# A hybrid attention layer whose kernel schedules itself: the schedule learns of the port that VectorE and GpSimd share, and its TensorE prices are set anew

## The chip, the cores and the metric

The kernel runs on one core of one Trainium2 chip. Its engines are TensorE (PE in the profile, its weight loads PEld), VectorE (DVE), ScalarE (ACT), GpSimd (POOL) and SyncE (SP), which issues the DMAs. Each engine works through its own list of instructions in order and waits for others through semaphores. The metric is device microseconds of one execution, the median of the runs shown.

## What is computed

One decoder layer over 512 tokens of 1024 features, in fp32. Cut to what matters here:

```python
h = rmsnorm(x, ln_mix_g)
dq, dk, dv, nq, kc, vc, ksl, vsl, kwn, vwn, ng, mg = split(h @ w_in)
dq, dk, nq, ksl, kwn = (rope(rmsnorm(z)) for each)
y_diff = rmsnorm((softmax(q0 k0) - lam * softmax(q1 k1)) @ v)          # 8 heads, causal
k_cmp, v_cmp = (gelu(blocks(z + pos) @ w1) @ w2 for z in (kc, vc))     # 31 blocks
y_nsa = g0 * att(nq, k_cmp, v_cmp) + g1 * att(nq, ksl, vsl) + g2 * att(nq, kwn, vwn)   # 16 heads
mixed = sigmoid(mg0) * (y_diff @ w_proj_diff) + sigmoid(mg1) * (y_nsa @ w_proj_nsa)
x = x + mixed @ w_out
x = x + square(relu(rmsnorm(x) @ w_mlp_up)) @ w_mlp_down
```

## The kernel before

**Work and tiles.** Every large product is done with operands split in two: `hi` is the value rounded to fp32r and `lo` the remainder, and a product is three matmuls, hi·hi, hi·lo and lo·hi. Weights come in 157 pieces of 128 x 1024 (tile `wraw`, by DMA). `WStream.get` (L372) splits each piece in halves of 512 columns: a copy writes `whi` (ACT or DVE, whichever is free first by the schedule), and a subtraction writes `wlo` (DVE or POOL, likewise). Pieces are split one ahead of their use and loaded two ahead.

**Stages.** The input is normalised and transposed (`hn`, `hTh`, `hTl`). Then four streams run at once with a filler: `rope_stream` (L873) normalises and turns queries and keys (`norm_rope`, L811: tiles `sqr`, `str`, `t1r`, `t2r`, `rw`), transposes them on PE (`ptp`) and splits them; `score_stream` (L1014) makes scores (`sb`), maxima and exponentials (`p`, statistics `sm` and `smn`); `value_stream` (L1146) transposes probabilities (`pta`, `ptn`), splits them (`ah`, `al`) and multiplies them with values (`av`, `avn`); a side stream does the compressed keys and values (`hb`, `ob`). The filler writes the large projections (`gb`, weights stationary or moving), one chunk after the other. After the attention come the projections, the output product and the MLP, in banks `gb` and `ga` in turn.

**What sets the order.** Nothing is issued while the kernel is written out. Each call is noted by `Sched.note` (L190) with what it reads and writes, the engines that could do it, and a price in ns for each (`price`, L163). `Pe.run` (L72) takes steps of the streams by falling priority and advances its own clock `pe.now` by the price of each matmul (`mm`, L438, and `tr`, L442). At the end `Sched.flush` (L256) plays a list schedule: a clock for each engine, and at each step the engine that could start first takes, of what is ready, the instruction of the highest priority. An instruction with two possible engines goes to the one that gets to it first. The instructions are then issued in the order of the planned starts, so these prices decide both each engine's order and who does the splits. The step that takes an instruction is

```python
p, op = heapq.heappop(ok[e])
op.eng = e
op.start, op.end = t, t + op.ways[e][1]
self.free[e] = op.end
```

In it each engine's clock is its own: no instruction of one engine makes another's take longer. Nearly every instruction is issued from one line of `flush`, so the profile names them by their tiles; all have line L326.

Of the kernel before, what the change touches and what calls it, by code (L numbers as in the profile page):

```python
# [26 lines left out]
# how long (ns) a result of other engines takes to be there  # L27
S_LAT, P_LAT, T_LAT = 1000, 4000, 2000
# how much later (ns) than usual it may come without holding up what was put after it
SLACK = 250  # L30
# what a task yields at the end of a piece of weights
PIECE = 1e-3

# columns of w_in
# [4 lines left out]
# columns of the table of shape constants  # L39
# [25 lines left out]
class Pe:  # L65
    """The tensor engine's clock (ns) as the kernel is written out: its instructions are issued in the order
    written, so a task is written on when what it waits for should be there."""
# [4 lines left out]
    def run(self, tasks):  # L72
        """tasks: generators by falling priority. They yield a time to wait (ns), or a condition."""
# [20 lines left out]
class Engine:  # L94
    """Takes down the instructions of one engine."""
# [9 lines left out]
class Pool:  # L105
    """A tile pool whose buffers the schedule knows."""
# [20 lines left out]
class Op:  # L127
    __slots__ = ("eng", "ways", "a", "k", "prio", "deps", "users", "bufs", "left", "ready", "start", "end", "dma")


class Sched:
    """Instructions are taken down in the order the kernel is written, with what each reads and writes. A clock
    per engine and the usual price of each instruction then say which goes next: of those that are ready the one
    that is hot, then the one written first. In this order they are issued."""
# [5 lines left out]
    def __init__(self, nc):  # L140
        self.nc, self.tiles, self.ops, self.hot = nc, {}, [], False
        self.engs = {"ACT": nc.scalar, "DVE": nc.vector, "POOL": nc.gpsimd}
        self.free = {e: 0.0 for e in ("PE", "ACT", "DVE", "POOL", "SP")}
        self.hw = self.dma = 0.0
        self.count = 0
        self.held, self.queue = {}, {}
# [3 lines left out]
    def lat(self, p, c, reads):  # L150
        """from the end of p to the start of c; reads: c reads what p has written"""
# [11 lines left out]
    def price(self, eng, method, aps, k):  # L163
# [4 lines left out]
        if eng == "PE":  # L168
            if method == "transpose":
                return 109.0  # L170
            return max(107.0, 3 + self.size(aps[-1]) * 0.4167)
# [17 lines left out]

    def note(self, ways, a, k):  # L190
        """ways: engine, method and its function, of each engine that could do it"""
# [5 lines left out]
        op.ways = {e: (fn, self.price(e, m, aps, k)) for e, m, fn in ways}  # L197
        op.dma = None
# [57 lines left out]
    def flush(self):  # L256
        """issues what has been taken down"""
# [33 lines left out]
        while len(done) < len(ops):  # L291
# [14 lines left out]
            p, op = heapq.heappop(ok[e])  # L306
            op.eng = e
            op.start, op.end = t, t + op.ways[e][1]
# [21 lines left out]
class When:  # L330
    """Something that is there from a time on."""
# [11 lines left out]
class Slots:  # L343
    """Buffers of a pool: taken only when the last reader of an older one is written out."""
# [17 lines left out]
class WStream:  # L362
    """Weights in the order of use: loaded two pieces ahead, split one piece ahead."""
# [32 lines left out]
def hybrid_block(ctx: ExitStack, tc: tile.TileContext, x, ln_mix_g, w_in, dqg, dkg, lq1, lk1, lq2, lk2,  # L396
# [25 lines left out]
    # ------------------------------------------------------------------ helpers  # L422
# [8 lines left out]
    def split(hi, lo, src, hi_engs=("ACT", "DVE"), lo_engs=("DVE",)):  # L431
        """src = hi + lo, each short enough for one pass of the tensor engine"""
# [5 lines left out]
    def mm(out, lhsT, rhs, n, start, stop):  # L438
        T.matmul(out, lhsT=lhsT, rhs=rhs, start=start, stop=stop)
        pe.now += max(107.0, n * 0.4219)  # L440

    def tr(out, src):  # L442
        T.transpose(out, src, ident)
        pe.now += 109.0
# [3 lines left out]
    def rows(w, c0, n=512):  # L448
        """pieces of 256 rows, n columns from c0"""
# [5 lines left out]
    def segs(w, c0, strides, n):  # L455
        """pieces of 256 rows, runs of n columns from c0, at the strides ((stride, count), ...) from each other"""
# [15 lines left out]
    def gemm_tm(banks, xh, xl, nk=KT, mark=False, by_bank=0, n=512, per=2):  # L472
        """banks[t] = x[t] @ w ; x given as lhsT slices [128 k, 128 tokens], w n wide, per slices of k a piece;
        the last by_bank pieces bank by bank"""
# [1138 lines left out]
```

## Time and profile before

| what | value |
|---|---|
| median of 3 runs | 1117.32 us |
| the three runs | 1117.01 to 1119.86 us |
| profiled execution, first to last instruction | 1117.1 us |
| PE busy, share of the span | 1066.3 us, 95% |
| DVE busy | 802.3 us, 72% |
| ACT busy | 464.9 us, 42% |
| POOL busy | 415.4 us, 37% |
| mean granted TensorE clock | 0.997 |

How to read it: the busy time of an engine is the union of its instructions' times. A matmul's end is modelled and overlaps the next one's start, so a busy PE is not yet one that issues as fast as it can. The engines work on stages with different limits, so a share over the whole span says little; the windows by stage and the waits say more. The profiled execution is 0.2 us from the median of the runs, so its sums can be held against that median.

### The profile page before, as it was taken

What the parts mean: (1) busy time and instruction counts of PE and PEld (TensorE: products, weight loads), DVE (VectorE), ACT (ScalarE), POOL (GpSimd) and SP (SyncE); (2) the same over time, 40 slices, a digit from 0 to 9 for tenths busy, and PEclk for the clock granted to TensorE, in tenths of its full rate; (3) what the DMA queues carried; (4) which work ended last, traced back from release to release, by engine and by line L of the source; (5) the groups of instructions that cost most, each with busy time, mean ns of one, the idle gap of its engine ahead of it and who ended that gap; (6) DMA issues with size and microseconds to landing.
All of it is one profiled execution on the core that took longest, in us unless ns stands there. A gap on an engine that the chain in (4) does not pass through costs nothing.

```text
span 1117.1 us, 15775 instructions
## 1 busy us (share of the span) xinstructions
PE 1066.3 (95%) x5257; PEld 873.5 (78%) x5257; DVE 802.3 (72%) x1961; ACT 464.9 (42%) x1132; POOL 415.4 (37%) x416
## 2 busy tenths in 40 slices
PE   6999989999899999999999999999999999999998
PEld 5777867779677778777788887787888888888887
DVE  7788599999888999999999998657454233445232
ACT  4256245655454365565465564313332111233110
POOL 3714478338647271073211112322322222222321
PEclk9999999999999999999999999999999999999999
DMA  6354355542653324526345344642322233333232
GB/s 206 97 148 118 113 151 149 152 129 71 164 153 94 85 69 132 142 85 199 122 134 170 100 155 134 225 138 90 94 94 95 95 98 104 101 95 95 94 132 75
DMA packets 83905, 136.76 MB, mean 122 GB/s; under 512 B 8816, under 2 KB 33904, under 8 KB 83824
## 3 DMA queue, kind: packets, MB, share of 16 engines
q1 hardware_dynamic: 83824, 135.77, 40.2%
q8 instruction: 41, 0.67, 0.3%
q14 instruction: 40, 0.33, 0.1%
HBM read 106.64 MB, written 14.42 MB: 108 GB/s over the span
## 4 chain that ended last, share of the span: by engine, by line
PE 62%; DVE 22%; POOL 5%; DMA 5%; issue 3%; ACT 2%; SPq 1%; DVEq 0%; ACTq 0%; POOLq 0%
PE gb L326 31%; PE ga L326 21%; DVE p L326 5%; PE sb L326 3%; DMA kk<-kp 3%; PE avn L326 3%; DVE wlo L326 2%; POOL str L326 2%; PE ptn L326 2%; DVE al L326 2%; DVE rw L326 1%; DVE t1r L326 1%; POOL t1r L326 1%; DMA wraw<-in_w_in_dram 1%; PE hb L326 1%
## 5 line engine op out<-in xcount | busy, mean ns | idle before, releaser
L326 POOL TENSOR_TENSOR wlo<-wraw,whi 128x512 fp32r<-128x512 f32 (+1 forms) x163 | 237.7, 1461 | 596.8 <-ACT whi L326 386.9
L326 ACT CAST whi<-wraw 128x512 fp32r<-128x512 f32 (+1 forms) x203 | 121.8, 618 | 327.6 <-PE gb L326 158.5
L326 DVE CAST whi<-wraw 128x512 fp32r<-128x512 f32 x111 | 49.9, 451 | 198.2 <-PE ga L326 87.1
L326 DVE TENSOR_TENSOR wlo<-wraw,whi 128x512 fp32r<-128x512 f32 x151 | 130.4, 865 | 8.6 <-ACT whi L326 2.2
L326 PE MATMUL gb<-whi,hTh 128*128 128x512 f32 (+2 forms) x352 | 133.5, 388 | 2.2 <-ACT hTh L326 1.3
L326 PE MATMUL gb<-wlo,hTh 128*128 128x512 f32 (+2 forms) x352 | 135.1, 385 | 0.0
L326 PE MATMUL gb<-whi,hTl 128*128 128x512 f32 (+2 forms) x352 | 134.5, 383 | 0.4 <-DVE hTl L326 0.4
L326 DVE CUSTOM_DVE_ANT_0 p<-sb,cst 128x512 f32<-128x512 f32 (+2 forms) x192 | 91.8, 480 | 4.5 <-PE sb L326 3.3
L326 ACT ACTIVATE p<-p,smn 128x512 f32<-128x512 f32 (+3 forms) x128 | 71.9, 562 | 34.6 <-DVE smn L326 33.8
L326 PEld LDWEIGHTS gb<-whi,hTh 128*128 128x128 f32 x352 | 67.1, 192 | 12.5 <-ACT hTh L326 1.8
L326 PEld LDWEIGHTS gb<-whi,hTl 128*128 128x128 f32 x352 | 67.3, 192 | 10.8 <-DVE hTl L326 1.4
L326 PEld LDWEIGHTS gb<-wlo,hTh 128*128 128x128 f32 x352 | 67.6, 192 | 9.4 <-DVE wlo L326 0.3
L326 PE MATMUL gb<-big,whi 128*128 128x512 f32 x192 | 66.9, 407 | 0.0
L326 DVE TENSOR_SCALAR p<-p,smn,gates 128x512 f32<-128x512 f32 (+3 forms) x128 | 65.4, 515 | 1.5
L326 ACT CAST ah<-ptn 128x128 fp32r<-128x128 f32 (+3 forms) x101 | 42.8, 427 | 54.5 <-PE ptn L326 43.8
L326 PE MATMUL gb<-hTh,whi 128*128 128x512 f32 x160 | 64.6, 404 | 0.6 <-DVE t0t L326 0.4
L326 PE MATMUL gb<-hTl,whi 128*128 128x512 f32 x160 | 64.9, 406 | 0.0
L326 PE MATMUL ptn<-cst,p 128*128 128x128 f32 x320 | 60.4, 276 | 4.5 <-DVE al L326 1.4
L326 PE MATMUL gb<-hTh,wlo 128*128 128x512 f32 x160 | 64.5, 405 | 0.0
L326 PE MATMUL ga<-h2h,whi 128*128 128x512 f32 x160 | 62.4, 391 | 0.5 <-DVE x L326 0.5
L326 PE MATMUL ga<-h2l,whi 128*128 128x512 f32 x160 | 62.5, 390 | 0.0
L326 PE MATMUL ga<-h2h,wlo 128*128 128x512 f32 x160 | 62.2, 390 | 0.0
(250 smaller groups left out, 2631.5 us busy)
## 6 DMA issues: line engine op xcount, KB each, us to landing
wraw<-in_w_in_dram SPq DMA_DIRECT2D x36, 512.0 KB, 3.6
wraw<-in_w_mlp_up_dram SPq DMA_DIRECT2D x32, 512.0 KB, 3.8
wraw<-in_w_mlp_down_dram SPq DMA_DIRECT2D x32, 512.0 KB, 3.6
kk<-kp SPq DMA_DIRECT2D x48, 256.0 KB, 4.5
wraw<-in_w_in_dram SPq DMA_DIRECT2D x36, 256.0 KB, 3.1
big<-yd SPq DMA_DIRECT2D x16, 512.0 KB, 4.0
yd<-yo SPq DMA_DIRECT2D x8, 512.0 KB, 3.2
wraw<-in_w_proj_diff_dram SPq DMA_DIRECT2D x8, 512.0 KB, 3.8
```

Of the source, the lines that this page charges most:

```text
L326: op.ways[op.eng][0](*op.a, **op.k)
```

## The change

The schedule gets a sixth clock, `self.port`. A new function `ported` names the instructions that hold the SBUF port which DVE and POOL share: on POOL all but powers, on DVE four methods when no operand is in PSUM, and neither when all operands are under 64 elements wide. In `flush` an instruction that holds the port and finds it taken is put off: the next ready instruction of that engine that doesn't need the port goes first, and if there is none, the first starts when the port is free. The prices of PE in `price`, and the same in `mm` and `tr` for `pe.now`, become those of the second set of numbers. All else of the diff takes out comments and docstrings, whose lines stay blank or go, so that the line of the issued instructions is L357 in the kernel after.

```diff
@@ class Sched
-        self.hw = self.dma = 0.0
+        self.hw = self.dma = self.port = 0.0
...
             if method == "transpose":
-                return 109.0
-            return max(107.0, 3 + self.size(aps[-1]) * 0.4167)
+                return 113.0
+            return max(113.0, 5.5 + self.size(aps[-1]) * 0.4315)
...
+    TWICE = ("tensor_tensor", "tensor_scalar", "scalar_tensor_tensor", "tensor_copy")
+
+    def ported(self, eng, method, aps, k):
+
+        if max(self.size(x) for x in aps) < 64:
+            return False
+        if eng == "POOL":
+            return k.get("op") != OP.pow
+        return eng == "DVE" and method in self.TWICE and not any(
+            self.tiles[x.tensor.name].space == "PSUM" for x in aps if x.tensor.name in self.tiles)
...
             p, op = heapq.heappop(ok[e])
+            if op.port[e] and self.port > t:
+                put_off = [(p, op)]
+                while ok[e] and put_off[-1][1].port[e]:
+                    z = heapq.heappop(ok[e])
+                    if z[1].left == 0:
+                        put_off.append(z)
+                if not put_off[-1][1].port[e]:
+                    p, op = put_off.pop()
+                else:
+                    p, op = put_off.pop(0)
+                for z in put_off:
+                    heapq.heappush(ok[e], z)
             op.eng = e
-            op.start, op.end = t, t + op.ways[e][1]
+            op.start = max(t, self.port) if op.port[e] else t
+            op.end = op.start + op.ways[e][1]
+            if op.port[e]:
+                self.port = op.end
             self.free[e] = op.end
...
     def mm(out, lhsT, rhs, n, start, stop):
         T.matmul(out, lhsT=lhsT, rhs=rhs, start=start, stop=stop)
-        pe.now += max(107.0, n * 0.4219)
+        pe.now += max(113.0, 5.5 + n * 0.4315)
```

The set of instructions is the same; their order and some of their engines are not. Counted in the two built programs:

| instruction | before | after |
|---|---|---|
| `wlo` halves of 512: DVE / POOL | 149 / 162 | 98 / 213 |
| of these in pieces 0 to 84 (up to the second projection of the attention's results): DVE / POOL | 79 / 91 | 38 / 132 |
| `whi` halves of 512: DVE / ACT | 110 / 201 | 100 / 211 |
| of `whi`, halves of any width, in pieces 0 to 84: DVE | 43 | 29 |
| `t1r<-t1r,t2r` 128x512: DVE / POOL | 16 / 8 | 8 / 16 |
| `t1r<-rw,ropec` 128x512: DVE / POOL | 4 / 4 | 0 / 8 |
| copies `rw<-gb` 128x512: DVE / ACT | 12 / 16 | 7 / 21 |
| `ah<-ptn`, all widths: DVE / ACT | 27 / 101 | 38 / 90 |

**PE in the fourth rope job** (the differential queries and keys of the last chunk; `rw_727` to `rw_730` are its four token tiles, `ptp` the transposes, `gb` the filler's products with the key chunk's weights `whi_767` and `whi_782`). Before:

```order
L326 MATMUL ptp_788<-cst_129,rw_729 128x128
...
L326 MATMUL gb_778<-whi_767,hTh_68 128x256
L326 MATMUL gb_778<-wlo_768,hTh_68 128x256
L326 MATMUL gb_778<-whi_767,hTl_69 128x256
L326 MATMUL ptp_785<-cst_129,rw_730 128x128
L326 MATMUL ptp_788<-cst_129,rw_730 128x128
L326 MATMUL gb_779<-whi_767,hTh_68 128x256
```

After:

```order
L357 MATMUL ptp_788<-cst_129,rw_729 128x128
...
L357 MATMUL gb_780<-whi_782,hTl_69 128x256
L357 MATMUL gb_781<-whi_782,hTh_68 128x256
L357 MATMUL gb_781<-wlo_783,hTh_68 128x256
L357 MATMUL ptp_785<-cst_129,rw_730 128x128
L357 MATMUL ptp_788<-cst_129,rw_730 128x128
L357 MATMUL gb_781<-whi_782,hTl_69 128x256
```

The transposes of the last token tile moved behind more of the filler: 24 other matmuls stand between them and those of the third tile before, and 55 after, among them 11 with the chunk's next piece of weights.

**POOL in the first rope job** (`wlo` are halves of weights, `t1r` and `t2r` the two products of the rotation, `str` the statistics: `epsc` adds a constant, `mhalf` takes the power -1/2). Before:

```order
L326 TENSOR_TENSOR wlo<-wraw,whi 128x512 x4
L326 TENSOR_TENSOR t1r<-rw,ropec 128x256
L326 TENSOR_TENSOR t2r<-rw,ropes 128x4x32 x3
L326 TENSOR_TENSOR t1r<-rw,ropec 128x256
L326 TENSOR_TENSOR str<-str,epsc 128x8
L326 TENSOR_TENSOR t1r<-t1r,t2r 128x512
L326 TENSOR_TENSOR str<-str,mhalf 128x8
```

After:

```order
L357 TENSOR_TENSOR wlo<-wraw,whi 128x512 x6
L357 TENSOR_TENSOR t1r<-rw,ropec 128x256 x2
L357 TENSOR_TENSOR t2r<-rw,ropes 128x4x32
L357 TENSOR_TENSOR str<-str,epsc 128x8
L357 TENSOR_TENSOR wlo<-wraw,whi 128x512
L357 TENSOR_TENSOR str<-str,mhalf 128x8
```

Two more halves of weights moved to POOL ahead of the job, and one stands inside it, ahead of the first power.

**DVE in the same job** (`whi` and `wlo` are halves of weights, `rw` a token tile). Before:

```order
L326 CAST whi<-wraw 128x512
L326 TENSOR_TENSOR wlo<-wraw,whi 128x512
L326 CAST whi<-wraw 128x512
L326 TENSOR_TENSOR wlo<-wraw,whi 128x512
L326 COPY rw<-gb 128x512
L326 TENSOR_TENSOR t2r<-rw,ropes 128x4x32
L326 TENSOR_TENSOR t1r<-rw,ropec 128x256
L326 TENSOR_REDUCE str<-sqr 128x8
```

After:

```order
L357 CAST whi<-wraw 128x512
L357 TENSOR_TENSOR wlo<-wraw,whi 128x512
L357 COPY rw<-gb 128x512
L357 TENSOR_TENSOR t2r<-rw,ropes 128x4x32
L357 TENSOR_REDUCE str<-sqr 128x8
L357 TENSOR_TENSOR t2r<-rw,ropes 128x4x32
L357 CAST whi<-wraw 128x512
L357 TENSOR_TENSOR t2r<-rw,ropes 128x4x32
```

One `whi` and one `wlo` left the place ahead of the tile's copy, and the sum `str` comes ahead of the rest of the rotation.

## Rows read from the trace of the kernel before

**Rows 1.** Page: busy time by engine, then the span in 40 slices.
```profile
PE 1066.3 (95%) x5257; PEld 873.5 (78%) x5257; DVE 802.3 (72%) x1961; ACT 464.9 (42%) x1132; POOL 415.4 (37%) x416
DVE  7788599999888999999999998657454233445232
```

**Rows 2.** Windows by stage: length, busy of each engine (instructions), granted clock, DMA.
```profile
0.00:20.00 20.00, 10.76 (x45) 8.37 (x46) 11.98 (x20) 10.59 (x18) 6.23 (x13) 1.00 0.67 229
20.00:680.00 660.00, 624.14 (x3304) 510.63 (x3303) 592.50 (x1639) 350.21 (x928) 284.62 (x324) 0.99 0.44 128
770.00:1080.00 310.00, 310.00 (x1369) 256.44 (x1368) 124.50 (x197) 72.24 (x125) 88.68 (x57) 1.00 0.31 100
```

**Rows 3.** Waits of PE, 20 to 680 us: who, total us, times, longest.
```profile
PE ptp L326 <- DVE rw L326: 8.1, 6, 4.7
PE sb L326 <- DVE smn L326: 5.5, 11, 1.3
PE sb L326 <- DVE sm L326: 3.3, 8, 1.1
PE av L326 <- DVE yt L326: 2.1, 4, 0.7
```

**Rows 4.** Page: the chain that ended last, shares of the span by engine.
```profile
PE 62%; DVE 22%; POOL 5%; DMA 5%; issue 3%; ACT 2%; SPq 1%; DVEq 0%; ACTq 0%; POOLq 0%
```

**Rows 5.** Timeline at 604 to 612 us: start, us, engine, instruction, idle before.
```profile
605.10 0.48 DVE L326 TENSOR_SCALAR p<-p,smn,gates 128x384 f32<-128x384 f32 x1
...
606.93 0.43 DVE L326 CAST whi<-wraw 128x512 fp32r<-128x512 f32 x1 [0.91 <-PE gb L326]
...
607.49 1.33 POOL L326 TENSOR_TENSOR wlo<-wraw,whi 128x512 fp32r<-128x512 f32 x1 [8.77 <-PE gb L326]
...
607.59 1.78 DVE L326 TENSOR_TENSOR wlo<-wraw,whi 128x512 fp32r<-128x512 f32 x1
...
610.04 0.62 PE L326 MATMUL sb<-kk,qa 128*128 128x384 f32 x2 [0.57 <-DVE smn L326]
```

**Rows 6.** Timeline at 274 to 285 us, DVE, POOL and PE.
```profile
274.44 4.85 POOL L326 TENSOR_TENSOR t1r<-rw,ropec 128x256 f32<-128x256 f32 x1
...
276.87 0.68 DVE L326 TENSOR_TENSOR wlo<-wraw,whi 128x512 fp32r<-128x512 f32 x1
...
282.73 1.73 DVE L326 TENSOR_TENSOR rw<-t1r,str 128x512 f32<-128x512 f32 x1 [4.03 <-POOL t1r L326]
...
284.52 0.66 PE L326 MATMUL ptp<-cst,rw 128*128 128x128 f32 x2 [4.71 <-DVE rw L326]
```

**Rows 7.** Windows around that wait.
```profile
280.00:284.50 4.50, 0.00 (x0) 0.00 (x0) 1.77 (x2) 0.00 (x0) 4.50 (x4) 1.00 0.12 45
284.50:288.00 3.50, 3.48 (x17) 3.48 (x18) 3.50 (x7) 1.64 (x3) 1.09 (x1) 0.51 0.34 77
```

**Rows 8.** Timeline of PE at 290 to 292 us: products 256 wide.
```profile
291.49 0.28 PE L326 MATMUL gb<-whi,hTh 128*128 128x256 f32 x1
291.61 0.28 PE L326 MATMUL gb<-wlo,hTh 128*128 128x256 f32 x1
```

**Rows 9.** Groups of DVE by shape, 20 to 680 us: count, busy, mean ns.
```profile
L326 DVE TENSOR_TENSOR wlo<-wraw,whi 128x512 fp32r<-128x512 f32 x69 | 63.0, 916 | 2.8 <-issue 1.5 <-ACT whi L326 0.4
L326 DVE TENSOR_TENSOR rw<-t1r,str 128x512 f32<-128x512 f32 x24 | 21.2, 882 | 7.4 <-POOL t1r L326 6.6 <-POOL str L326 0.7
L326 DVE TENSOR_SCALAR p<-p,smn,gates 128x384 f32<-128x384 f32 x32 | 17.9, 561 | 0.4
L326 DVE TENSOR_TENSOR t1r<-t1r,t2r 128x512 f32<-128x512 f32 x16 | 14.6, 911 | 0.2 <-POOL t2r L326 0.2
L326 DVE COPY rw<-gb 128x512 f32<-128x512 f32 x12 | 8.2, 685 | 6.6 <-PE gb L326 6.5
L326 DVE TENSOR_TENSOR al<-ptn,ah 128x384 fp32r<-128x384 f32 x31 | 16.9, 546 | 0.1
```

**Rows 10.** Groups of POOL by shape, 20 to 680 us.
```profile
L326 POOL TENSOR_TENSOR wlo<-wraw,whi 128x512 fp32r<-128x512 f32 x86 | 117.9, 1375 | 304.4 <-ACT whi L326 182.4 <-DVE whi L326 54.2 <-PE gb L326 25.9
L326 POOL TENSOR_TENSOR str<-str,mhalf 128x8 f32<-128x8 f32 x24 | 43.1, 1798 | 0.2
L326 POOL TENSOR_TENSOR sm<-sm,mhalf 128x1 f32<-128x1 f32 x32 | 20.4, 637 | 2.0
L326 POOL TENSOR_TENSOR t1r<-t1r,t2r 128x512 f32<-128x512 f32 x8 | 11.6, 1453 | 1.4 <-DVE t2r L326 1.3
L326 POOL TENSOR_TENSOR str<-str,mhalf 128x4 f32<-128x4 f32 x8 | 8.5, 1057 | 0.0
```

**Rows 11.** Timeline at 42 to 50 us, POOL powers and DVE beside them.
```profile
44.98 3.69 POOL L326 TENSOR_TENSOR str<-str,mhalf 128x8 f32<-128x8 f32 x2
...
47.72 1.28 DVE L326 TENSOR_TENSOR wlo<-wraw,whi 128x512 fp32r<-128x512 f32 x2
```

**Rows 12.** Windows of 40 us: the stretch in which POOL is busiest.
```profile
160.00:200.00 40.00, 37.41 (x193) 29.82 (x194) 38.90 (x92) 22.77 (x53) 30.17 (x35) 1.00 0.58 161
```

More of the change, by code (lines that the diff above doesn't have):

```diff
@@ L127 @@
 class Op:
-    __slots__ = ("eng", "ways", "a", "k", "prio", "deps", "users", "bufs", "left", "ready", "start", "end", "dma")
+    __slots__ = ("eng", "ways", "a", "k", "prio", "deps", "users", "bufs", "left", "ready", "start", "end", "dma",
+                 "port")
 class Sched:
@@ L197, in note @@
         op.ways = {e: (fn, self.price(e, m, aps, k)) for e, m, fn in ways}
+        op.port = {e: self.ported(e, m, aps, k) for e, m, _ in ways}
         op.dma = None
@@ L439, in mm @@
         T.matmul(out, lhsT=lhsT, rhs=rhs, start=start, stop=stop)
-        pe.now += max(107.0, n * 0.4219)
+        pe.now += max(113.0, 5.5 + n * 0.4315)
     def tr(out, src):
         T.transpose(out, src, ident)
-        pe.now += 109.0
+        pe.now += 113.0
     ws = WStream(wp, split)
```

## The prediction

> **What bounds the kernel now.** I read the busy times first. PE is busy for 95% of the span, DVE for 72%, but DVE's slices stand mostly at eight and nine tenths for the first 25 of 40 and at two to six after that [rows 1]. So there are two stages, and the windows price them. From 770 to 1080 us PE is busy for all of 310.00 us: nothing the schedule does to DVE or POOL can be had back there. From 20 to 680 us PE is idle for 660 - 624.1 = 35.9 us while DVE is busy for 592.5 us, 90% [rows 2]. That is the stage to argue about. Who PE waits for there: the first four rows of its waits, 19.0 us, all name DVE (the rotated tiles `rw`, the statistics `smn` and `sm`, the sums `yt`) [rows 3]. The chain that ended last says the same: 62% PE, 22% DVE, 5% POOL [rows 4]. Before 20 us the order is nearly the same in both kernels; I count nothing there.
>
> Next, why DVE is late. At 607.59 us a 128x512 subtraction of DVE takes 1.78 us; a like one at 276.87 takes 0.68. POOL had begun its own subtraction 0.10 us earlier, for 1.33 us, and DVE's ends 0.55 us after POOL's: it stood still for 1.1 us, and PE then waited 0.57 us for the next statistics [rows 5, 6]. It goes the other way too: at 274.44 POOL's product of 256 takes 4.85 us, with DVE subtracting weights meanwhile; DVE then sits 4.03 us for POOL's result and PE 4.71 us for DVE's [rows 6]. The schedule of before knows of neither.
>
> **The change, part by part.**
>
> *PE's place in the fourth rope job.* Between the transposes of its third and fourth tile stand 24 other matmuls before and 55 after. In the trace this is the place of the 4.71 us wait [rows 6]. The 31 added ones are 256 wide and follow each other every 0.12 us [rows 8]: 31 x 0.12 = 3.7 us of cover. The wait costs more than itself: in the 3.5 us behind it the granted clock is 0.51, the level of 1.2 GHz, after PE had been idle from 280 to 284.5 us [rows 7]; 3.5 x 0.49 = 1.7 us. Bounds: 0, if the tile is as much later as PE's place is, to 4.7 + 1.7 = 6.4. I take 3.7 + 1.7 = 5.4, as the order there covers most of it.
>
> *Work that leaves DVE, up to the second projection (pieces 0 to 84).* 41 `wlo` halves x 0.68 us [rows 6] = 27.9; 14 `whi` casts x 0.43 [rows 5] = 6.0; 12 products and sums of the rotation, 512 wide, x 0.68 = 8.2 (an estimate by the subtraction of that size); 5 copies `rw` x 0.685 [rows 9] = 3.4. What it gets: 11 casts `ah`, of which the view shows only the subtraction next to them, 0.546 at a width of 384 [rows 9]: 6.0. Net 39.5 us of 592.5. What of it lies on the path: DVE makes 22% of the chain, 246 us of its 802 busy [rows 1, 4], 0.31 us for each one busy; 39.5 x 0.31 = 12.2 us. Bounds: 0, if other work of DVE or lock waits fill the room, to 35.9 - 4.7 = 31.2, all other idle time of PE in the stage.
>
> *Lock waits of DVE.* Means over the undisturbed time: `wlo` 69 x (0.916 - 0.68) = 16.3 us, `rw` 24 x (0.882 - 0.68) = 4.8, `t1r` 16 x (0.911 - 0.68) = 3.7, `p` of 384 wide 32 x (0.561 - 0.48) = 2.6 [rows 5, 6, 9]: 27.4 us in four groups. The 41 moved halves take 41 x 0.236 = 9.7 of it with them. The new rule lets DVE do work from PSUM while POOL holds the port and places the rest behind it. I take half of the 27.4 as gone, 13.7 x 0.31 = 4.2 us. Bounds: all gone, 8.5; or a third more of it, -2.8 (below).
>
> *Work that comes to POOL.* 41 halves x 1.375 + 12 x 1.453 [rows 10] = 73.8 us, onto an engine that is idle for 660 - 284.6 = 375 us of the stage [rows 2]. By its part in the chain, 5% of 1117.1 or 56 us of its 415 busy [rows 1, 4], each costs 0.13: 9.9 us. But 304.4 us of POOL's idle time lie just before `wlo`, waiting for `whi` [rows 10]: those halves start when they can and are not queued. The cover is the piece that is split ahead of its use. Between 0 and -9.9 I take -3, nearer to the free end.
>
> *PE's prices.* They alone take nothing from any engine. They make the planned PE slower against the others, so the plan puts results that PE waits for nearer to their use, against what the port does; what the two make together is the order shown. Counted in PE's order the last product of the attention's values stands 31 matmuls later than before, so on balance DVE gets more time, not less. No DMA is added, and weights stay loaded two pieces ahead; zero for SP's queue.
>
> *After 680 us.* The split goes from 4 and 4 halves to 3 and 5 in most MLP chunks; PE is full there [rows 2], the idle engines hide it: zero.
>
> Sum against the profiled execution: 5.4 + 12.2 + 4.2 - 3 = 18.8 us; 1117.1 - 18.8 = 1098.3, and 0.2 for the median: **1098.5 us**.
>
> *A rule against the change.* `ported` says that powers don't hold the port. From 44.98 to 48.67 us POOL does two powers, and beside the second DVE's two subtractions of weights, from 47.72 on, take 1.28 us together, undisturbed [rows 11]. The Trainium skill (SBUF — State Buffer, section Who interferes with whom) says that a DVE instruction with two SBUF inputs contends with a GpSimd instruction that reads SBUF, and that the loser blocks until the other's whole instruction is done. By that, the powers would hold it too, 43.1 + 20.4 + 8.5 = 72.0 us of POOL's 284.6 [rows 2, 10], a quarter which the new schedule would still not know; with a quarter less of the gain the sum would be 1117.3 - 14.1 = 1103. The trace doesn't agree for powers, and I stay with it.
>
> **The rivals.**
>
> *More than that.* Where DVE falls behind once, all that queues behind it is late, so one removed wait may remove several. If all visible idle time of PE in the stage went, 1117.3 - 35.9 = 1081 us. For it: nearly all those waits name DVE [rows 3]. Against: 10% of DVE's time is still idle only because it waits for others, and such chains stay.
>
> *The plan is not kept.* Planned turns at the port hold only while every engine runs to the ns; a late DMA moves them, and the 4.85 us row shows that POOL gets no turn while DVE issues without a break [rows 6]. Then chance rules: POOL's work that holds the port grows from 284.6 - 72.0 = 212.6 to 286 us, 32% to 43% of the stage; DVE's waits grow from 27.4 to about 36.5, the -2.8 above, and POOL's cost is the full 9.9. 12.2 - 2.8 - 9.9 = -0.5: 1117 to 1118, with the fourth rope job's gain 1112: no change, or a gain of less than half a per cent.
>
> *Slower: POOL becomes the late engine.* A power of a rope job now stands behind a half of weights, as in the first job's order. Eight jobs end in a last tile whose transposes PE must do in its place. Each meets one or two such halves: 8 x 1.375 x 1.5 = 16.5 us, less the fourth job's 5.4: 1117.3 + 11 = 1128 us. It decides from the point where POOL has no idle time left in a rope stretch. Its fullest has 30.2 us busy of 40 [rows 12]; up to five halves are added to one chunk, 6.9 us: 37, still under 40. So it is unlikely, but the rope job's order speaks for it.
>
> **How the numbers follow.** Forecast, 1088 to 1108: 0.48. More, below 1088: 0.20. The plan is not kept, 1108 to 1121: 0.20, of which 0.09 below 1114. Slower by POOL, above 1121: 0.12. A difference of 0.3% (3.4 us) is about what a measurement of this kernel can tell from no change; that makes 1114 and 1120.7 the borders: faster 0.48 + 0.20 + 0.09 = 0.77, same 0.11, slower 0.12. The range 1079 to 1120 leaves out the lowest third of the second case and the last.
>
> **What would show it.** Right: in the stage up to the last product of the values PE's idle time falls from 35.9 to some 20 us; DVE's `wlo` mean comes below 0.80 us with fewer than 1.5 us long; the wait of `ptp` for `rw` loses its 4.7 us and the clock stays at 2.4 GHz behind it. Wrong: `wlo` on POOL takes PE's waits over (PE or PEld waiting for POOL), `str` on POOL stands in front of `rw`, DVE's mean of two-input work is as long as before, or PE waits for DVE as long at other tiles. If DVE's busy time falls by 40 us and the span doesn't, the share of 0.31 was the wrong step.

## The result and the profile after

The kernel after takes 1107.25 us (median of 4 runs, 1105.2 to 1109.28), the kernel before 1117.62 in the same rounds. The ratio of the two (here and below: the time over that of the kernel before in the same rounds) is 0.9896, with a 95% interval of 0.9878 to 0.9914: 10.4 us faster, inside the range, and 8.8 us short of the 1098.5 that was forecast. The profiled execution spans 1107.5 us. It is the longest of the four runs, with a mean granted clock of 0.989; the shortest, 1105.2 us, has 0.995.

First the page of the kernel after, against [rows 1, 4]: busy times, DVE's 40 slices, and the chain that ended last.

```profile
PE 1061.3 (96%) x5257; PEld 881.4 (80%) x5257; DVE 769.9 (70%) x1899; ACT 462.0 (42%) x1125; POOL 490.3 (44%) x485
...
DVE  7678498899888999999999897655543223345232
...
PE 74%; DVE 11%; DMA 6%; POOL 4%; issue 2%; SPq 1%; ACT 1%; DVEq 0%; ACTq 0%; POOLq 0%
```

DVE lost 32 us of busy time and half of its share of the chain, and POOL gained 75 us. The windows of the kernel after by stage, against [rows 2] (length, busy time of each engine with its instructions, granted clock, DMA share, GB/s):

```profile
20.00:680.00 660.00, 632.18 (x3367) 528.36 (x3365) 577.60 (x1592) 356.50 (x941) 343.78 (x382) 0.99 0.45 130
680.00:770.00 90.00, 84.18 (x374) 68.42 (x375) 58.69 (x88) 25.60 (x51) 35.29 (x23) 0.96 0.44 144
770.00:1080.00 310.00, 309.99 (x1368) 256.38 (x1367) 115.07 (x190) 67.52 (x113) 100.14 (x65) 1.00 0.31 100
```

In the stage from 20 to 680 us PE does 63 more matmuls (3304 before) and is idle for 27.8 us, not 35.9. From 770 on nothing changed. The surprise is the middle row. The prediction had put zero there, and PE is idle for 5.8 us of it. A finer cut shows where the 10 us come from and go. Windows of the kernel before, then of the kernel after:

```profile
0.00:640.00 640.00, 595.21 (x3134) 486.43 (x3135) 568.27 (x1547) 336.31 (x881) 286.65 (x333) 0.99 0.45 130
640.00:720.00 80.00, 78.25 (x380) 62.75 (x378) 69.70 (x153) 39.02 (x92) 19.43 (x13) 1.00 0.49 156
```
```profile
0.00:640.00 640.00, 605.73 (x3218) 506.47 (x3219) 554.99 (x1517) 344.69 (x901) 342.65 (x389) 0.99 0.46 134
640.00:720.00 80.00, 72.44 (x340) 58.63 (x338) 62.62 (x125) 34.52 (x78) 25.66 (x18) 0.96 0.50 164
```

By 640 us PE has done 84 matmuls more than before, and from 640 to 720 it does 40 fewer. The 44 that are left are matmuls of the full stage; from 770 to 1080 us one takes 309.99 / 1368 = 0.2266 us, so they are worth 10.0 us, and that is the 9.6 us between the two spans. Such counts return in all the runs below. They are a rough measure ahead of 720 us, where matmuls differ in width. Weighed by width (each matmul of the trace at the new price that the schedule has for it), PE is 16.8 us of work ahead by 640 us (569.5 us against 552.7), and 7.3 us go back from 640 to 720 (68.0 against 75.3).

Why PE falls behind there: the timeline of the kernel after at 680 to 687 us, POOL, DVE and PE (start, us, engine, instruction, idle time before), and windows over the same place.

```profile
680.56 3.14 POOL L357 TENSOR_TENSOR wlo<-wraw,whi 128x512 fp32r<-128x512 f32 x2
...
680.80 1.77 DVE L357 TENSOR_TENSOR tm<-tm 128x512 f32<-128x512 f32 x1
...
682.49 2.35 DVE L357 SCALAR_TENSOR_TENSOR kk<-tm,kk 128x512 fp32r<-128x512 f32 x2
...
685.37 0.68 DVE L357 TENSOR_TENSOR big<-yr,big 128x512 fp32r<-128x512 f32 x1
...
686.10 0.80 PE L357 MATMUL ga<-big,whi 128*128 128x512 f32 x1 [4.00 <-DVE big L357]
```
```profile
684.00:686.00 2.00, 0.00 (x0) 0.00 (x0) 2.00 (x4) 0.00 (x0) 0.47 (x1) 0.50 0.71 198
686.00:690.00 4.00, 3.90 (x9) 3.16 (x10) 0.75 (x3) 1.13 (x2) 1.18 (x1) 0.50 0.82 273
```

POOL's two subtractions of weights hold up DVE's `tm` (1.77 us; 0.69 at 717.8 us) and the first of the two 128x512 sums of `kk` behind it (2.35 together; one at 684.2 us takes 0.68). The split of the last results (`big`) comes behind them, and PE waits 4.00 us for it. Some 2.1 us of this are the hold-up; the rest is DVE's own order, in which `big` stands behind four other instructions. The granted clock is 0.50, the level of 1.2 GHz, at the end of the wait and behind it until 690 us. PE has nothing else to do there: in its order 1860 matmuls stand behind the attention's last product of values, in the kernel before 1891. The work that covered this place before has been spent on the earlier stretches. The filler's last product with the input starts at 634.1 us, 659.4 before, and the first projection of the attention's results (`gb<-big`) is over at 679.9 us. In the kernel before it goes on until 692.5 us, and this window shows PE full there:

```profile
680.00:690.00 10.00, 9.95 (x46) 7.77 (x45) 7.88 (x10) 3.29 (x7) 3.16 (x2) 1.00 0.33 105
```

The clock works against the change in other places too. In the profiled runs it is granted at 0.50 for 23.9 us ahead of 720 us in the kernel after (from 154.4, 168.0, 191.9, 523.0 and 683.4 us on), and for 6.8 us in the kernel before (from 110.5 and 284.6 on). At half the clock these 17.1 us more cost at most some 8.5 us of PE's work, by which the gain could be larger.

The waits of PE from 20 to 680 us in the kernel after, against [rows 3] (total us, times, longest):

```profile
PE av L357 <- DVE yt L357: 2.3, 2, 1.5
PE ptp L357 <- DVE qb L357: 2.2, 2, 1.6
PE sbc L357 <- DVE qa L357: 2.0, 1, 2.0
PE sb L357 <- DVE sm L357: 1.9, 3, 1.0
...
PE gb L357 <- POOL wlo L357: 1.5, 2, 0.9
...
PE hb L357 <- POOL wlo L357: 1.2, 1, 1.2
```

The 8.1 us for `rw` and the 5.5 us for `smn` are gone from the head of the list; POOL's `wlo` is new in it with 2.7 us. And the groups of DVE and POOL over the same window, against [rows 9, 10] (count, busy us, mean ns, idle time before):

```profile
L357 DVE TENSOR_TENSOR wlo<-wraw,whi 128x512 fp32r<-128x512 f32 x31 | 28.1, 910 | 0.8 <-ACT whi L357 0.4 <-issue 0.2
L357 DVE TENSOR_TENSOR rw<-t1r,str 128x512 f32<-128x512 f32 x24 | 22.0, 918 | 5.3 <-POOL t1r L357 4.8 <-POOL str L357 0.5
L357 DVE TENSOR_SCALAR p<-p,smn,gates 128x384 f32<-128x384 f32 x32 | 18.4, 575 | 0.2
L357 DVE TENSOR_TENSOR t1r<-t1r,t2r 128x512 f32<-128x512 f32 x8 | 8.3, 1032 | 0.5 <-POOL t2r L357 0.5
```
```profile
L357 POOL TENSOR_TENSOR wlo<-wraw,whi 128x512 fp32r<-128x512 f32 x126 | 168.9, 1352 | 253.2 <-ACT whi L357 147.9 <-DVE whi L357 42.4 <-PE gb L357 37.2
L357 POOL TENSOR_TENSOR t1r<-t1r,t2r 128x512 f32<-128x512 f32 x16 | 22.1, 1379 | 1.4 <-DVE t2r L357 1.3
```

The work moved as forecast (38 `wlo` halves left DVE, 41 were forecast). But the instructions that stayed wait for the port as long as ever: `wlo` 910 ns (916 before), `rw` 918 (882), `t1r` 1032 (911), `p` 575 (561). With more work on POOL, the schedule that knows the port did not make DVE meet POOL less.

So two theories stood at the start of the experiments. (The plan is what `flush` works out ahead of issuing anything: an engine and a start for each instruction.) **Engines**: the gain is the work that left DVE, as the prediction had it. **Turns**: it is the order that the port's clock makes, above all how much PE does ahead of what waits for DVE. A third, **prices**, gives it to PE's new prices.

### The profile page after: what moved, and what is told of

The parts are those of the page before. It is cut to its first block, busy times and chain, and to the rows that moved or that the text cites. A ratio compares the mean times of both kernels' runs of the same rounds, so it can differ in the third digit from the quotient of the medians.

```text
span 1107.5 us, 15713 instructions
## 1 busy us (share of the span) xinstructions
PE 1061.3 (96%) x5257; PEld 881.4 (80%) x5257; DVE 769.9 (70%) x1899; ACT 462.0 (42%) x1125; POOL 490.3 (44%) x485
## 4 chain that ended last, share of the span: by engine, by line
PE 74%; DVE 11%; DMA 6%; POOL 4%; issue 2%; SPq 1%; ACT 1%; DVEq 0%; ACTq 0%; POOLq 0%
PE gb L357 38%; PE ga L357 21%; PE sb L357 4%; PE avn L357 3%; PE ptn L357 3%; DMA kk<-kp 2%; DVE p L357 2%; PE hb L357 2%; POOL wlo L357 1%; PE av L357 1%; DVE st L357 1%; POOL str L357 1%; SPq L357 1%; DVE big L357 1%; POOL t1r L357 1%
## 5 line engine op out<-in xcount | busy, mean ns | idle before, releaser
L357 POOL TENSOR_TENSOR wlo<-wraw,whi 128x512 fp32r<-128x512 f32 (+1 forms) x214 | 305.3, 1436 | 523.4 <-ACT whi L357 350.2
L357 ACT CAST whi<-wraw 128x512 fp32r<-128x512 f32 (+1 forms) x213 | 127.6, 617 | 353.2 <-PE gb L357 172.6
L357 DVE CAST whi<-wraw 128x512 fp32r<-128x512 f32 (+1 forms) x101 | 45.8, 454 | 208.2 <-PE ga L357 96.1
L357 PE MATMUL gb<-wlo,hTh 128*128 128x512 f32 (+2 forms) x352 | 135.4, 386 | 2.8 <-POOL wlo L357 1.5
L357 PE MATMUL gb<-whi,hTl 128*128 128x512 f32 (+2 forms) x352 | 134.6, 383 | 0.0
L357 PE MATMUL gb<-whi,hTh 128*128 128x512 f32 (+2 forms) x352 | 131.1, 392 | 1.8 <-ACT hTh L357 1.2
L357 DVE CUSTOM_DVE_ANT_0 p<-sb,cst 128x512 f32<-128x512 f32 (+2 forms) x192 | 91.7, 480 | 9.6 <-PE sb L357 8.9
L357 DVE TENSOR_TENSOR wlo<-wraw,whi 128x512 fp32r<-128x512 f32 (+2 forms) x100 | 82.7, 828 | 4.8 <-ACT whi L357 0.7
L357 ACT ACTIVATE p<-p,smn 128x512 f32<-128x512 f32 (+3 forms) x128 | 71.9, 562 | 33.1 <-DVE smn L357 32.5
L357 PEld LDWEIGHTS gb<-wlo,hTh 128*128 128x128 f32 x352 | 67.4, 191 | 14.6 <-POOL wlo L357 3.1
L357 PEld LDWEIGHTS gb<-whi,hTh 128*128 128x128 f32 x352 | 67.4, 194 | 13.3 <-ACT hTh L357 1.6
L357 PEld LDWEIGHTS gb<-whi,hTl 128*128 128x128 f32 x352 | 67.3, 191 | 10.2 <-DVE hTl L357 0.3
L357 DVE TENSOR_SCALAR p<-p,smn,gates 128x512 f32<-128x512 f32 (+3 forms) x128 | 68.8, 546 | 0.9
L357 PE MATMUL gb<-big,whi 128*128 128x512 f32 x192 | 67.2, 404 | 0.0
L357 PE MATMUL gb<-hTl,whi 128*128 128x512 f32 x160 | 64.8, 405 | 0.0
L357 DVE TENSOR_TENSOR al<-ptn,ah 128x128 fp32r<-128x128 f32 (+3 forms) x128 | 61.0, 481 | 4.8 <-ACT ah L357 2.2
L357 PE MATMUL gb<-hTh,whi 128*128 128x512 f32 x160 | 64.3, 403 | 0.0
L357 PE MATMUL gb<-hTh,wlo 128*128 128x512 f32 x160 | 63.5, 404 | 0.0
L357 PE MATMUL ga<-h2l,whi 128*128 128x512 f32 x160 | 62.4, 390 | 0.0
L357 PE MATMUL ga<-h2h,whi 128*128 128x512 f32 x160 | 62.4, 391 | 0.0
L357 PE MATMUL ga<-h2h,wlo 128*128 128x512 f32 x160 | 62.3, 389 | 0.0
L357 PE MATMUL ptn<-cst,p 128*128 128x128 f32 x320 | 58.4, 276 | 2.3 <-DVE al L357 0.8
```

The costliest lines, as they stand in the source:

```text
L357: op.ways[op.eng][0](*op.a, **op.k)
```

## Experiments: engines, turns and prices

Three of the first four runs (e1, e3, e4) and the kernel after form a square: the plan knows the port or not, and the choice of engine is that of the kernel after or that of the plan without port.

**Prices alone** (e1). The kernel after, with no instruction holding the port in the plan:

```diff
-        op.port = {e: self.ported(e, m, aps, k) for e, m, _ in ways}
+        op.port = {e: False for e, m, _ in ways}
```

> The kernel after, but no instruction holds the port in the plan: only TensorE's prices are new. The plan gives DVE 28 operations more than before, not fewer (472 of 1254 with a choice, before 444, after 382). Theory 'engines' (the 10.4 us are work that left DVE): slower than before, 1118 to 1126. Theory 'turns' (they are the order that the port's clock makes: results planned later, more products of TensorE ahead of them): about as before, 1114 to 1120, with the wait of the fourth rope job still there. Theory 'prices': 1107, as after.

Measured: 1137.74 us, ratio 1.0176 (1.0157 to 1.0194), 19.4 us slower than before. The new prices are the truer ones (a matmul 512 wide costs 226.4 ns in them and 216.4 in the old ones; the full stage above shows 226.6), and alone they make the kernel slower, by more than any of the three theories had. DVE has 28 more operations, but it isn't fuller: it is busy for 799.6 us in all, against 802.3 before.

**Port alone** (e2). The kernel after with PE's old prices, in `price`, `mm` and `tr`:

```diff
-                return 113.0
-            return max(113.0, 5.5 + self.size(aps[-1]) * 0.4315)
+                return 109.0
+            return max(107.0, 3 + self.size(aps[-1]) * 0.4167)
...
-        pe.now += max(113.0, 5.5 + n * 0.4315)
+        pe.now += max(107.0, n * 0.4219)
...
-        pe.now += 113.0
+        pe.now += 109.0
```

> The kernel before with the port's clock, TensorE at its old prices: DVE has 363 of the operations with a choice (after 382, before 444), and 59 matmuls stand ahead of the last tile of the fourth rope job. 'Engines': as after or better, 1103 to 1108. 'Turns': as after, 1105 to 1109. 'Prices': 1115 to 1119, as before.

Measured: 1103.05 us, ratio 0.9860 (0.9844 to 0.9875). It is the fastest of all runs, 15.3 us faster than before, at the lower end of what "engines" had and 2 us below "turns". "Prices" falls by these two runs.

**Engines without turns** (e3). No port in the plan, and every operation that has a choice is given the engine that it has in the kernel after, from a list:

```diff
+GIVEN = iter("...")            # the engine of each operation with a choice, as noted
...
+        if len(ways) > 1:
+            given = next(GIVEN)
+            ways = [x for x in ways if x[0][0] == given]
+            op.eng = ways[0][0]
...
-        op.port = {e: self.ported(e, m, aps, k) for e, m, _ in ways}
+        op.port = {e: False for e, m, _ in ways}
```

> Each operation is on the engine that it has in the kernel after, but the plan knows no port: nothing is put off or started later for it. TensorE's new prices. 'Engines': 1106 to 1110, the whole gain, though the order is another. 'Turns': 1114 to 1120, the gain is gone. If both have a part: 1111 to 1114. DVE's lock waits should be longer than in the kernel after by 'turns' (over 93 us), no longer by 'engines'.

Measured: 1144.25 us, ratio 1.0234 (1.0206 to 1.0261), the slowest of all, and far above what any theory had. Its waits of PE from 20 to 680 us, and its windows to 640 and 720 us:

```profile
PE ptp L377 <- DVE rw L377: 17.1, 8, 6.3
PE sb L377 <- DVE sm L377: 9.1, 9, 2.3
PE ptp L377 <- DVE kp L377: 4.6, 3, 2.0
```
```profile
0.00:640.00 640.00, 575.78 (x2995) 470.61 (x2996) 529.22 (x1428) 320.68 (x847) 328.36 (x380) 0.98 0.43 125
640.00:720.00 80.00, 79.29 (x414) 65.75 (x414) 64.72 (x184) 45.64 (x114) 21.26 (x16) 1.00 0.41 130
```

The same work is on the same engines as in the kernel after, and over the whole run DVE is as busy (772.3 us against 769.9). By 640 us it has been busy for less (529.2 us against 555.0), since it has got less done, as has PE: 223 matmuls less, or 42.4 us of work weighed by width. What is missing is not DVE's time; PE stands in front of `rw` and `sm` again. DVE's lock waits over the whole run, counted as in the section on the prediction below, are 88.5 us against 92.7 in the kernel after: not longer, as "turns" had expected.

**Turns without engines** (e4). The edit of e3 with the list of e1's engines, and the port kept in the plan.

> The opposite: the plan knows the port, but each operation is on the engine that the plan without port gave it (that of the kernel with the prices alone, DVE 472 operations). 'Engines': 1116 to 1126, since DVE is as full as in that kernel. 'Turns': 1105 to 1110. Both: between that kernel and the one after.

Measured: 1112.69 us, ratio 0.9945 (0.9927 to 0.9964), between e1 and the kernel after, where the case for both had put it. The square in us:

| | engines of e1 | engines of after |
|---|---|---|
| plan without port | 1137.74 (e1) | 1144.25 (e3) |
| plan with port | 1112.69 (e4) | 1107.25 (after) |

Read down, the port in the plan is worth 25.1 and 37.0 us. Read across, the engines are worth -6.5 and +5.4 us, either not much more than the 4.5 us by which neighbouring plans differ (c2 below). "Engines" falls as the main cause.

Does the port in the plan win its time by making the two engines meet less? With the engines of e1 they do meet less. DVE's groups over the whole run, e1, then e4:

```profile
L357 DVE TENSOR_TENSOR wlo<-wraw,whi 128x512 fp32r<-128x512 f32 x138 | 115.8, 841 | 6.1 <-ACT whi L357 1.2
L357 DVE TENSOR_TENSOR rw<-t1r,str 128x512 f32<-128x512 f32 x24 | 24.3, 1012 | 1.2 <-POOL str L357 1.1
```
```profile
L377 DVE TENSOR_TENSOR wlo<-wraw,whi 128x512 fp32r<-128x512 f32 x138 | 105.0, 762 | 7.4 <-ACT whi L377 2.9
L377 DVE TENSOR_TENSOR rw<-t1r,str 128x512 f32<-128x512 f32 x24 | 18.2, 757 | 1.3 <-POOL t1r L377 1.0 <-POOL str L377 0.2
```

The lock waits up to the end of the attention fall from 61.7 us in e1 to 49.7 in e4. With the engines of the kernel after they don't (70.7 us in e3, 73.3), and there the port's clock is worth more. So fewer lock waits can be a part of the 25.1 us, but they do not make the 37.0.

## Experiments: what the port's clock does

Does the plan have to know which instructions meet? Or is it enough that it counts DVE and POOL as slower than it did (**margin**), so that more products stand ahead of what waits for them?

**Dear without port** (e5). The kernel of e3 with its prices raised, so that either engine gets as much planned time in all as with the port:

```diff
-        op.ways = {e: (fn, self.price(e, m, aps, k)) for e, m, fn in ways}
+        op.ways = {e: (fn, self.price(e, m, aps, k) * {"DVE": 1.2, "POOL": 1.13}.get(e, 1.0)) for e, m, fn in ways}
```

> The kernel of e3 (engines as in the kernel after, no port in the plan, 1144.3 us), but with every planned price of DVE times 1.20 and of POOL times 1.13, which gives either engine the same planned time in all as the port's waits do (DVE 624.6 + 126.7 us, POOL 418.2 + 53.2). The plan does not know which instruction meets which. Theory 'turns' (the plan must place the two engines' instructions around each other): 1135 to 1145. Theory 'margin' (it is enough that the plan counts DVE as slower, as it is, and puts more products of TensorE ahead of what waits for it): 1104 to 1112.

Measured: 1134.89 us, ratio 1.0133 (1.0103 to 1.0162). The same planned time, spread evenly, wins 9.4 of the 37.0 us, and the time is just below what "turns" had. As much margin as this, by itself, is not the cause.

**No put-off** (e6). The kernel after without the rule that takes another ready instruction first; the block between `heappop` and `op.eng = e` goes, planned starts still stand behind the port:

```diff
-            if op.port[e] and self.port > t:
-                put_off = [(p, op)]
...
-                for z in put_off:
-                    heapq.heappush(ok[e], z)
             op.eng = e
```

> The kernel after without the rule that takes another ready instruction first while the port is held; starts are still planned behind the port. 'Turns', with the put-off as their core: 1115 to 1130. 'Margin': 1104 to 1111, since the planned time of DVE stays as long.

Measured: 1124.22 us, ratio 1.0044 (1.0029 to 1.0059). The rule is worth 17.0 us. Windows of this kernel:

```profile
0.00:640.00 640.00, 602.96 (x3142) 499.14 (x3143) 544.36 (x1447) 340.70 (x887) 329.37 (x387) 0.98 0.46 133
640.00:720.00 80.00, 69.30 (x341) 54.78 (x341) 67.48 (x167) 41.14 (x104) 19.99 (x14) 0.98 0.36 115
```

Against the kernel after 76 matmuls are missing by 640 us, and the stretch behind it is as thin (341): the filler is spent just as early, with less gained for it.

**More slack** (e7): `SLACK = 250` becomes `SLACK = 500` in the kernel after.

> The kernel after with SLACK, which the plan adds to every step from one engine to another, at 500 ns in place of 250. 'Margin' says that TensorE's dearer prices cost 4.2 us (1107.3 against 1103.05 of the port alone) because they take margin away, and that SLACK gives it back: 1100 to 1105. If the prices cost by some other turn of the order: 1106 to 1112. If more slack only fills buffers longer: over 1112.

Measured: 1129.65 us, ratio 1.0090 (1.0075 to 1.0106). **TensorE still cheaper** (e8): e2 with each of its PE prices times 0.95.

> The port's clock with TensorE's old prices times 0.95: still further from the trace than those of before (1103.05 us). 'Margin', not yet used up: 1098 to 1102. Used up: 1102 to 1106. 'True prices are best': over 1106.

Measured: 1118.87 us, ratio 0.9993 (0.9980 to 1.0006). Both ways to give more margin lose: 12 and 22 us against the kernel after, 16 and 27 against e2. Each fell into the last case that was named for it, against "margin"; but that true prices are best, as e8's last case says, is not what e1 and e2 show. From 640 to 720 us PE does 324 and 311 matmuls in them, the fewest of all. In e8 PE has done as much work by 640 us as in the kernel after (569.6 us against 569.5, weighed by width) and 10.6 us less from there to 720; its last filler product starts at 622.5 us, not 634.1. There the larger margin only spends the filler sooner. In e7 less is done in both stretches (562.9 and 58.8 us).

**Powers hold the port** (p1). The kernel after, with GpSimd's powers as holders in the plan, which is the rule that the prediction had weighed against the change:

```diff
+        if eng == "POOL" and k.get("op") == OP.pow:
+            return True
         if max(self.size(x) for x in aps) < 64:
```

> The kernel after, but in the plan GpSimd's powers hold the port too, whatever their width. The plan's own clock ends TensorE at 1093.5 us (that of the kernel after: 1061.6, and the chip 45.9 us later; the four other kernels that know of the port or count DVE as dear at the new prices end 45 to 55 us behind their plans, but with SLACK at 500 36.5). Theory 'the plan as lower bound, the chip some 46 us behind an honest one': if powers do not hold the port on the chip, the plan waits for nothing 32 us longer, and so does the chip: 1130 to 1145. If they do hold it (the rule that was weighed against the change): the chip comes nearer to its plan, 1100 to 1115.

Measured: 1121.07 us, ratio 1.0017 (1.0001 to 1.0033): 13.8 us slower than the kernel after, and between the two expected stretches, so its time settles neither. Its rows do. Timeline of POOL and DVE at 44 to 49 us:

```profile
44.10 1.64 POOL L359 TENSOR_TENSOR str<-str,mhalf 128x8 f32<-128x8 f32 x1
...
47.12 1.65 POOL L359 TENSOR_TENSOR str<-str,mhalf 128x8 f32<-128x8 f32 x1
```
```profile
44.16 0.68 DVE L359 TENSOR_TENSOR wlo<-wraw,whi 128x512 fp32r<-128x512 f32 x1
44.77 0.41 DVE L359 TENSOR_TENSOR t1r<-rw,ropec 128x256 f32<-128x256 f32 x1
47.19 0.69 DVE L359 TENSOR_TENSOR rw<-t1r,str 128x512 f32<-128x512 f32 x1 [2.02 <-POOL t1r L359]
```

Three subtractions and products of DVE with both inputs in SBUF lie inside the two powers and take their undisturbed 0.68, 0.41 and 0.69 us. At these places the powers do not hold DVE up, as [rows 11] had it.

**How far is chance?** Every number in the plan orders the instructions anew. Three runs change one that should mean nothing to the chip, `SLACK` by 10 ns:

> The kernel before with SLACK 260 ns in place of 250, which should mean nothing to the chip. Theory 'turns' (what the plan knows of the port is what tells the kernels apart): 1115 to 1121. Theory 'dice' (every change of a number orders the instructions anew, and such orders lie many us apart, whatever the plan knows): anywhere from 1105 to 1135; this one more than 5 us away from 1118.

> The kernel after with SLACK 240. 'Turns': 1104 to 1111. 'Dice': 1100 to 1130, more than 5 us from 1107. In its order of TensorE only 34 matmuls stand ahead of the last tile of the fourth rope job (after 57, before 30); if that place is worth its 5.4 us by itself, 1110 to 1113.

> The kernel after with SLACK 260; 34 matmuls at that place too. 'Turns': 1104 to 1111. 'Dice': 1100 to 1130, more than 5 us from 1107 and from the run with 240.

Measured: 1118.93 us (ratio 1.0003, 0.9994 to 1.0013), 1111.76 (0.9937, 0.9916 to 0.9958) and 1108.69 (0.9911, 0.9896 to 0.9926). The neighbours lie up to 4.5 us from their kernels; c2 lies 0.8 us above what "turns" had and nearer than "dice" had. The three kernels around the one after are all faster than the two around the one before, by 6 to 12 us, so the gain is the change's. Differences of some 5 us between two single plans can't be put down to what was changed: not the 4.2 us between e2 and the kernel after (by which the new prices would cost), nor the 5.4 us for the engines.

The two neighbours of the kernel after say something of the fourth rope job as well. Only 32 matmuls stand between the last two tiles in their traces (34 by the expectations' count), where the kernel after has 55. The time that c2's expectation named for the case that this place is worth its 5.4 us by itself, 1110 to 1113 us, is met by c2 and not by c3. In both traces PE does not wait for the last tile, and the granted clock is 1.00 from 280 to 292 us. So 32 cover this wait as 55 do.

## What the runs have in common

The plan keeps a clock of its own, and its last end on PE can be set beside the chip's. The table has, for each kernel, how long PE is idle in the plan, how far the profiled span ends behind that plan (with PE's work counted at the new prices everywhere, 1019.2 us, so the span is 1019.2 + the second column + the third), and PE's matmuls by 640 us and from there to 720.

| kernel | median us | PE idle in the plan, us | chip behind the plan, us | matmuls by 640 | 640 to 720 |
|---|---|---|---|---|---|
| before | 1117.6 | 15.8 | 82.1 | 3134 | 380 |
| c1 | 1118.9 | 16.4 | 84.7 | 3123 | 378 |
| e1 prices | 1137.7 | 15.7 | 105.3 | 3037 | 394 |
| e3 engines, no port | 1144.3 | 22.1 | 102.3 | 2995 | 414 |
| e5 dear, no port | 1134.9 | 60.7 | 47.6 | 3103 | 364 |
| e6 no put-off | 1124.2 | 59.2 | 45.3 | 3142 | 341 |
| e4 port, engines of e1 | 1112.7 | 41.9 | 49.7 | 3172 | 377 |
| c2 | 1111.8 | 37.2 | 55.2 | 3188 | 358 |
| c3 | 1108.7 | 36.2 | 51.8 | 3198 | 359 |
| after | 1107.3 | 42.4 | 45.9 | 3218 | 340 |
| e2 port, old prices | 1103.1 | 50.9 | 31.5 | 3242 | 339 |
| p1 powers | 1121.1 | 74.3 | 29.2 | 3136 | 357 |
| e7 slack 500 | 1129.7 | 70.6 | 36.5 | 3162 | 324 |
| e8 PE at 0.95 | 1118.9 | 78.5 | 19.2 | 3200 | 311 |

A plan that leaves the lock waits out looks short and is kept badly: e3 is 102.3 us behind its own. Counting time for them brings the chip back to the plan: e5 is 47.6 behind. But the plan itself now idles for 60.7 us. The put-off is what fills that: from e6 to the kernel after no other rule changes (the choice of engine follows: DVE has 1882 instructions in e6, 1899 in the kernel after), the lateness is the same (45.3 and 45.9), and the plan's idle time falls by 16.8 us, the span by 16.2. At the other end p1, e7 and e8 plan so carefully that PE stands still on paper, and get back less lateness than they pay. These pairs (e3 and e5, e6 and after) each change one rule; over the whole list the two columns are a description of what the runs did and not a law. That e1 loses 19.4 us against the kernel before fits it: the old prices make PE too early in the plan, so more of its products stand ahead of a wait, a margin that the truer prices would take away. The table shows that the lateness grows (82.1 to 105.3); the reason was not tried in another way.

DVE's busy time does not order the kernels at all. Over the whole run it is 772.3 us in e3, the slowest, 751.2 in p1, 802.3 before and 767.5 in e2, the fastest.

## Why the prediction was right and where it was wrong

The time and the direction came out, the mechanism mostly did not. The largest term of the sum, 12.2 us, stood for a cause that the runs reject, and another, 4.2 us, had the wrong sign. That the time still fell inside the range, which is 41 us wide, is in good part luck. Point by point:

- **PE's place in the fourth rope job (5.4 us): right at its place.** Rows of the kernel after, DVE, then PE, then the windows, against [rows 6, 7]:

```profile
280.42 1.78 DVE L357 TENSOR_TENSOR rw<-t1r,str 128x512 f32<-128x512 f32 x1
```
```profile
283.12 0.38 PE L357 MATMUL ptp<-cst,rw 128*128 128x128 f32 x2
```
```profile
280.00:284.00 4.00, 4.00 (x36) 4.00 (x35) 4.00 (x7) 1.72 (x4) 2.92 (x3) 1.00 0.44 131
284.00:288.00 4.00, 4.00 (x36) 4.00 (x36) 3.97 (x5) 1.86 (x5) 1.47 (x2) 1.00 0.50 127
```

  The fourth tile's `rw` is still held up (1.78 us) and done at 282.20, but PE comes for it only at 283.12 and waits for nothing. The clock stays at 1.00 where it was 0.51. Without the 3.7 us of added products PE would have been there at about 279.4. This was the one place where the prediction read the gain from PE's order. Its 5.4 us were not measured by themselves, and that the whole gain is made of such places is argued, not shown.
- **Work that leaves DVE (12.2 us): the step that failed.** Up to the last product of values (684.4 us before, 674.8 after) DVE's undisturbed work fell by some 32 us, where 39.5 was forecast. But it is not worth 0.31 us for each. By the square it is worth between -6.5 and +5.4. The share of DVE in the chain of waits says who ended late last, not what less work on it would give. The prediction had named this itself as the wrong step if DVE's time fell by 40 us and the span did not; e3 comes nearest to that case, with 27.3 us less of DVE's busy time than e1 and a time 6.5 us longer.
- **Lock waits (4.2 us): wrong sign.** Counting as waiting what a DVE instruction takes above the undisturbed time of its group, plus 40 ns, they were 64.5 us before and 73.3 after, up to the end of the attention. (The undisturbed time is the one that a fifth of the group's instructions in the same run do not exceed.) The forecast mark, a `wlo` mean below 0.80 us, was missed at 0.91. The rival "the plan is not kept" had reckoned with 9.1 us more of them, and 8.8 came. Its premise was right and its time wrong: this plan was not kept turn for turn, and the kernel was faster all the same.
- **PE's prices (zero): not settled.** Alone they cost 19.4 us, with the port 4.2, which two neighbouring plans can differ by. Zero was no safe value: they do not touch another engine's work, but they set how early the plan believes PE to be.
- **POOL's cost (3 us): about right.** PE waits 2.7 us for POOL's `wlo` in the stage, none of which stood in its list before. What POOL costs by way of DVE is not in this number. The rival in which POOL becomes the late engine did not come: its fullest window of 40 us (120 to 160 us) holds 34.9 us of work, where 37 were reckoned.
- **After 680 us (zero): wrong.** PE's busy time from 680 to 770 fell from 88.01 us in the kernel before to 84.18, 3.8 us, and from 640 to 720 us 7.3 us of the lead were lost, since the filler that PE had been given earlier was no longer there for the attention's tail. The terms ahead sum to 18.8 us, and by 640 us PE was 16.8 us ahead. That these are near each other is chance, since the terms are wrong one by one. So the 7.3 us are near the 8.8 us that the forecast was off by, but the gap cannot be put down to this step alone; what the lower clock takes, at most some 8.5 us by the first section, is of the same size, and of the clock the sum had only the 1.7 us that the fourth rope job gives back.
- The mark for PE's idle time from 20 to 680 us, some 20 us, was missed at 27.8.

**What stays open.** Why the put-off orders the rest so well was not taken apart further: with the engines of the kernel after it does not make the two engines dodge each other on the chip. The port's clock changes the order of DVE, POOL and ACT along with that of PE, and no run changed one of them alone. That the gain lies in how much PE does ahead of what waits for DVE fits the waits and the counts, and is not shown. Whether the new prices of PE help or hurt beside the port would need several neighbouring plans of each. The version with the port and the old prices is faster than both kernels here (1103.05 us), by 15 us against the kernel before, and nothing shows that it would stay 4 us ahead of the kernel after under small changes.

## What to carry to other kernels

When a kernel's order comes from a plan, correct the plan's waits together: truer prices for one engine alone cost 19 us here, it seems because they took away a margin that had covered the errors of the others. An engine's share of the chain of waits is no price for its work; test it by moving the work with the order's rule left as it was. A filler is a stock: what is spent ahead of one wait is missing at the last one, so look first at the stretch where it runs out; and before a difference of 1% is explained, change a number of the plan that means nothing and see how far the time moves.

## What the runs showed of the hardware

GpSimd's powers (1.64 and 1.65 us for 128x8) left DVE's two-input work inside them undisturbed: 0.68 and 0.69 us for 128x512, 0.41 us for 128x256. GpSimd's subtractions do disturb it: DVE's 128x512 `tm` beside two `wlo` of POOL took 1.77 us, and 0.69 elsewhere. A plan that knows this lowered the sum of such waits with one choice of engines (61.7 us in e1, 49.7 in e4) and not with the other (70.7 in e3, 73.3 in the kernel after).
